# Moving the small tiles of a decoder layer so that its large SBUF tiles start at other byte offsets

## The chip, the cores and the metric

The kernel runs on one core of one Trainium2 chip. The metric is the device time of one execution in microseconds (us), the median over several runs. The kernel before takes 2655.73 us (median of three runs, 2654.69 to 2656.63).

## The reference, cut to what matters

One decoder layer on x (512 tokens of width 2048), in float32, with a memory of 256 rows:

```
q_a, k_a, v_a, q_b, k_b, v_b = split(h @ w_in)          # 2048 -> 1024+256+256+3*1024
o_a = sliding-window softmax attention with sinks (16 heads, 4 key heads)
o_b = stick-breaking attention (16 heads)
h   = layer_norm(ALPHA * h + concat(rmsnorm(o_a), rmsnorm(o_b)) @ w_o)
h   = layer_norm(ALPHA * h + cross_attention(h, mem))   # w_q_mem, w_kv_mem, w_o_mem
gate, up = split(h @ w_gate_up)                         # 2048 -> 2 * 5632
h   = layer_norm(ALPHA * h + (silu(gate) * up) @ w_down)
```

## The kernel before, in words

Nearly all of the work is matrix products on TensorE. Each float32 operand is kept as two tiles, a rounded high part and the rest (`split`, L122: ScalarE casts, VectorE subtracts), and each product is three matmuls: high with high, high with low, low with high (`mm3`, L144; `product`, L1037; `product_turned`, L1047). Every matmul loads a stationary operand of 128 by 128 (a LDWEIGHTS) and streams a moving operand of 256 or 512 columns. Each matmul has a load of its own, also where its neighbour has the same stationary operand: there are 16544 of either.

The stages follow each other in this order: the two value projections (from 0 us on), the two attentions with the query and key projections running between their pieces as filler (about 120 to 530 us), the projections of the memory (to about 730 us), the output projection (to 930 us), memory cross-attention (to about 1300 us), gate and up (L1055, to about 2190 us) and down (L1044, to the end). Gate-up and down use products of half-size blocks, seven for eight (`PRODUCTS`, L1077), with the blocks' sums made on VectorE. TensorE's and SyncE's orders are written out by hand; VectorE, ScalarE and GpSimd are ordered by the scheduler.

SBUF is laid out by pools, one after the other in the order in which they are opened (L69 to L75):

- `const`: the identity `ident`, the distances `dmt`, the block diagonal `bd`, and a few small ones.
- `px`: eight tiles of 8 KB per partition for tokens and blocks of them (x, the memory, the memory's values, h, blocks a11, a12, s4 and half of s2).
- `pm`, `pt`, `pg`: 14, 8 and 4 tiles of 4 KB (v, mix, probabilities, keys and queries, the other blocks, sums of weights).
- `pw`: nine tiles of 4 KB through which every weight passes: `ws` (as loaded), `wh` and `wl` (high and low).
- `sm`: the small tiles, that is maxima `mx`, negated maxima `nm`, sums `rs`, moments `mv`, statistics `bst`, and four `o` tiles of 2 KB.

In a product one operand of TensorE comes from `pw` (the weights) and the other from `px`, `pm`, `pt` or `pg` (the tokens). In the value, output, memory-output and down stages the tokens are stationary and the weights stream with 512 columns; in the query and key projections, the memory's projections, the key products and gate-up the weights are stationary and the tokens stream. The attention products (`avb`, `ava`, `zb`, `za`) take both operands from `pm`, `pt` and `pg`. The two matmuls of `norm` (L314, L315) are the only ones whose stationary operand, `bd`, comes from `const`.

Every slice that a matmul reads starts at a multiple of 128 floats, 512 bytes, within its tile. So where an operand starts, counted modulo 512 bytes, is a property of its pool. Before, `px`, `pm`, `pt`, `pg` and `pw` all start at 288 modulo 512, and `ident`, `dmt` and `bd` at 128.

Of the kernel before, what the change touches and what calls it, by code (L numbers as in the profile page):

```python
# [26 lines left out]
F32 = mybir.dt.float32  # L27
# [5 lines left out]
P = 128  # L33
# [24 lines left out]
def a_head(j, half):  # L58

    return 4 * (2 * (j // 4) + half) + j % 4  # L60
# [3 lines left out]
def layer(ctx, tc, io, out):  # L64
# [3 lines left out]
    PS = bass.MemoryType.PSUM  # L68
    const = ctx.enter_context(tc.tile_pool(name="const", bufs=1))  # L69
    px = ctx.enter_context(tc.tile_pool(name="px", bufs=4))  # L70
    pm = ctx.enter_context(tc.tile_pool(name="pm", bufs=14))
    pt = ctx.enter_context(tc.tile_pool(name="pt", bufs=2))
    pg = ctx.enter_context(tc.tile_pool(name="pg", bufs=4))
    pw = ctx.enter_context(tc.tile_pool(name="pw", bufs=3))
    sm = ctx.enter_context(tc.tile_pool(name="sm", bufs=2))  # L75
    banks = ctx.enter_context(ExitStack())
# [12 lines left out]
    def mtile(shape, name, dt=F32R):  # L89
        return pm.tile(shape, dt, tag="m", name=name)  # L90
# [6 lines left out]

    def otile(name, dt=F32):
        return sm.tile([P, 512], dt, tag="o", name=name, bufs=4)

    def f32(ap):
        return ap.bitcast(F32)

    def ps_z(name):
        return ps.tile([P, 2, 512], F32, tag="z", name=name, bufs=2)
# [20 lines left out]
    def urgent(f, *args, **kw):  # L126
        with tc.high_priority():
            f(*args, **kw)

    def stage(src, name):  # L130
        st = pw.tile([P, 1024], F32, tag="ws", name=f"{name}s")
        nc.sync.dma_start(st, src)
        return st
# [17 lines left out]
    def both(operands):  # L151

        heads = [operands(h, cs(h, 64)) for h in range(2)]
        for i, j in ((0, 0), (0, 1), (1, 0)):
            for acc, lhs, rhs in heads:
                nc.tensor.matmul(acc, lhs[i], rhs[j], start=(i, j) == (0, 0), stop=i == 1)

    def at(pair, *idx):
        return pair[0][idx], pair[1][idx]
# [3 lines left out]
    def cs(i, w):  # L163
        return slice(i * w, (i + 1) * w)
# [6 lines left out]
    bd = const.tile([P, P], F32R, name="bd")  # L171
    nsink = const.tile([P, 16], F32, name="nsink")
    gq = const.tile([P, 16], F32, name="gq")
    ones = const.tile([P, 1], F32, name="ones")
    nc.gpsimd.memset(ones, 1.0)

    def load_consts():
# [20 lines left out]
    for nb in range(2):  # L198
        acc = four_banks(nb, f"v{nb}")
        for u in range(8):  # L200
            if nb == 0 and u == 0:
                st, ws = pw.tile([P, 2, 512], F32, tag="ws", name="x0s"), pw.tile([P, 1024], F32, tag="ws", name="wvb0s")
# [7 lines left out]
            elif nb == 0:  # L210
                st = stage(io["xT"][u], f"x{u}").rearrange("p (c n) -> p c n", c=2)
# [177 lines left out]
    class Window:  # L389
# [6 lines left out]
        def scores(self):  # L396
            j, st = self.j, self.st
            q, k = proj["qa", j], proj["ka", j // 4]
            z = ps_z(f"za{j}_{st}")
            for b in range(2):  # L400
                n = 2 * st + b
                keys = slice(max(n - 1, 0) * P, max(n - 1, 0) * P + 256)
                both(lambda h, r: (z[:, h, cs(b, 256)], at(q, r, cs(n, P)), at(k, r, keys)))
            s = mtile([P, 2, 512], f"sa{j}_{st}", F32)
            s4 = s.rearrange("p h (b n) -> p (h b) n", b=2)
            for h in range(2):
                dist = dmt if st == 0 else dmt[:, 1:2].to_broadcast([P, 2, 256])
                slope = 2.0 ** (-8.0 * (a_head(j, h) + 1) / 16)
                nc.vector.scalar_tensor_tensor(
                    s[:, h].rearrange("p (b n) -> p b n", b=2), dist, -float(np.float32(slope)),  # L410
                    z[:, h].rearrange("p (b n) -> p b n", b=2), op0=ALU.mult, op1=ALU.add)
            mx = sm.tile([P, 4], F32, tag="mx", name=f"mx{j}_{st}")
            nm = sm.tile([P, 4], F32, tag="nm", name=f"nm{j}_{st}")
            rs = sm.tile([P, 4], F32, tag="rs", name=f"rs{j}_{st}")
            mx2 = mx.rearrange("p (h b) -> p h b", b=2)
            nm2 = nm.rearrange("p (h b) -> p h b", b=2)
            nc.vector.tensor_reduce(mx, s4, axis=AX.X, op=ALU.max)
            nsk = nsink[:, 2 * j:2 * j + 2].unsqueeze(2).to_broadcast([P, 2, 2])
            nc.vector.scalar_tensor_tensor(nm2, mx2, -1.0, nsk, op0=ALU.mult, op1=ALU.min)  # L419
            for i in range(4):  # L420
                nc.scalar.activation(s4[:, i], s4[:, i], AF.Exp, bias=nm[:, i:i + 1], accum_out=rs[:, i:i + 1])  # L421
            nc.vector.tensor_tensor(mx2, nm2, nsk, op=ALU.subtract)
            nc.scalar.activation(mx, mx, AF.Exp)
            nc.vector.tensor_tensor(rs, rs, mx, op=ALU.add)
            nc.vector.reciprocal(rs, rs)
            nc.vector.tensor_tensor(s4, s4, rs.unsqueeze(2).to_broadcast([P, 4, 256]), op=ALU.mult)
            self.s = s
# [265 lines left out]
    def ycol(t, nb):  # L693
        return y[t][nb // 2][:, cs(nb % 2, 512)]
# [4 lines left out]
    stats = {}  # L699

    def bn(name, t, nb):
        if (name, t) not in stats:
            stats[name, t] = sm.tile([P, 4, 6], F32, tag="bst", name=f"{name}st{t}", bufs=4)
        nc.vector.bn_stats(stats[name, t][:, nb], ycol(t, nb))

    for nb in range(4):
# [32 lines left out]
            y[t] = to  # L739

    def moments(t, name):
        mv = sm.tile([P, 4], F32, tag="mv", name=f"{name}mv{t}", bufs=4)
        nc.vector.bn_aggr(mv[:, 0:2], stats[name, t])
        mu, v, r0, r1 = (mv[:, i:i + 1] for i in range(4))
        nc.vector.tensor_scalar_add(v, v, LN_EPS)
        nc.scalar.activation(r0, v, AF.Ln)
        nc.scalar.activation(r0, r0, AF.Exp, scale=-0.5)
        nc.vector.scalar_tensor_tensor(r1, r0, v, r0, op0=ALU.mult, op1=ALU.mult)
        nc.vector.tensor_scalar(r1, r1, -0.5, 1.5, op0=ALU.mult, op1=ALU.add)
        nc.vector.tensor_tensor(r0, r0, r1, op=ALU.mult)  # L750
        return mu, r0

    def normalise(t, mu, r0, gb, shared, to):
        g, b = gb
        if shared:
            neg = sm.tile([P, 4], F32, tag="nm", name=f"neg{t}")[:, :1]
            nc.gpsimd.tensor_scalar_mul(neg, mu, -1.0)
        for nb in range(4):
            yc = ycol(t, nb)
            yn = to[nb // 2][:, cs(nb % 2, 512)] if to else yc  # L760
            gc, bc = g[nb // 2][:, cs(nb % 2, 512)], b[nb // 2][:, cs(nb % 2, 512)]
            if nb in shared:
                nc.scalar.activation(yn, yc, AF.Identity, bias=neg)
                nc.gpsimd.tensor_tensor(yn, yn, gc, op=ALU.mult)
                nc.scalar.mul(yn, yn, r0)
                nc.gpsimd.tensor_tensor(yn, yn, bc, op=ALU.add)
                continue
            nc.vector.scalar_tensor_tensor(yn, yc, mu, gc, op0=ALU.subtract, op1=ALU.mult)
            yield
            nc.vector.scalar_tensor_tensor(yn, yn, r0, bc, op0=ALU.mult, op1=ALU.add)  # L770
            yield
# [86 lines left out]
    def soft(hp, t, sc):  # L858

        sc = sc.rearrange("p (h m) -> p h m", h=2)  # L860
        pr = otile(f"pr{hp}_{t}").rearrange("p (h m) -> p h m", h=2)
        nm = sm.tile([P, 2], F32, tag="nm", name=f"mnm{hp}_{t}")
        rs = sm.tile([P, 2], F32, tag="rs", name=f"mrs{hp}_{t}")
        nc.vector.tensor_reduce(nm, sc, axis=AX.X, op=ALU.max)
        nc.vector.tensor_scalar_mul(nm, nm, -MEM_SCALE)
        for i in range(2):
            nc.scalar.activation(pr[:, i], sc[:, i], AF.Exp, bias=nm[:, i:i + 1], scale=MEM_SCALE,
                                 accum_out=rs[:, i:i + 1])
        nc.vector.reciprocal(rs, rs)
        nc.vector.tensor_tensor(pr, pr, rs.unsqueeze(2).to_broadcast([P, 2, M]), op=ALU.mult)  # L870

        def turn(tr):
            for i in range(2):
                for m in range(2):
                    nc.tensor.transpose(tr[:, cs(2 * i + m, P)], pr[:, i, cs(m, P)], ident)
            for i in range(2):
                h = 2 * hp + i
                if h not in pth:
                    pth[h], ptl[h] = mtile([P, 2, 512], f"pmh{h}"), mtile([P, 2, 512], f"pml{h}")
                urgent(split, pth[h][:, :, cs(t, P)], ptl[h][:, :, cs(t, P)],  # L880
                       tr[:, cs(i, 256)].rearrange("p (m n) -> p m n", m=2))
        return turn
# [115 lines left out]
    for half in range(2):  # L998
        for pair in range(2):
# [13 lines left out]
            for i in range(2):  # L1013
                for j in range(2):
                    t, nb = 2 * half + i, 2 * pair + j
# [308 lines left out]
    for i, kind in enumerate(block_kinds):  # L1324
# [15 lines left out]
        for place in order:  # L1340
            name, role = PRODUCTS[place]
# [108 lines left out]
```

## Time and profile before

| what | value |
|---|---|
| median of three runs | 2655.73 us |
| the profiled execution | 2657.68 us |
| its span, first to last instruction | 2655.9 us |
| TensorE (PE) busy | 2588.7 us, 97% |
| loads of the stationary operand (PEld) | 2329.7 us, 88%, beside PE |
| VectorE (DVE) busy | 1914.3 us, 72% |
| ScalarE (ACT) busy | 1193.5 us, 45% |
| DMA | 478.59 MB, mean 180 GB/s |

Matmuls are pipelined: the duration that a row gives for one is longer than the time until the next starts. What counts for the length of a stretch is the distance from one start to the next, called pitch below. It is read from the timeline, in which each row begins with a start in microseconds.

### The profile page before, as it was taken

The numbers are of one execution on the slowest core, as the hardware profiler recorded it, in microseconds if no ns is written. First come the engines' busy times: TensorE is split into PE (matmuls) and PEld (weight loads), VectorE is DVE, ScalarE is ACT, GpSimd is POOL, SyncE is SP. The second block draws the span as 40 slices with busy tenths as digits, with TensorE's granted clock in tenths as the row PEclk, the third lists the DMA queues.
The fourth block names the chain that finished last, engine by engine and source line by source line (L and its number), as shares of the span: only waits on it lengthen the run. The fifth ranks groups of instructions, "written<-read, shape, count | busy, mean of one in ns | idle before, by whom it ended". The sixth has DMA issues, their size and how long they took to land.

```text
span 2655.9 us, 40755 instructions
## 1 busy us (share of the span) xinstructions
PE 2588.7 (97%) x16544; PEld 2329.7 (88%) x16544; DVE 1914.3 (72%) x2170; ACT 1193.5 (45%) x1576; POOL 185.7 (7%) x324
## 2 busy tenths in 40 slices
PE   9999999999999999999999999999999998999995
PEld 7877777799988889988999999999999996877884
DVE  4258888997533574448797879887887777777788
ACT  3246656665421353334554444444445443333332
POOL 0001111010000000000000101010111001000001
PEclk9999999999999999999999999999999998999998
DMA  5322222245652483236755656563455577787763
GB/s 183 102 87 70 71 71 76 88 158 185 227 183 95 166 278 135 93 121 203 235 190 188 230 203 226 184 247 134 163 207 198 198 258 271 265 331 267 257 244 121
DMA packets 134747, 478.59 MB, mean 180 GB/s; under 512 B 16544, under 2 KB 16800, under 8 KB 133920
## 3 DMA queue, kind: packets, MB, share of 16 engines
q1 hardware_dynamic: 111024, 393.15, 42.8%
q0 software_dynamic: 23536, 82.85, 8.3%
q8 instruction: 129, 2.11, 0.3%
q14 instruction: 58, 0.48, 0.1%
HBM read 403.06 MB, written 72.88 MB: 179 GB/s over the span
## 4 chain that ended last, share of the span: by engine, by line
PE 75%; issue 12%; DVE 5%; DMA 4%; ACT 2%; POOL 1%; SPq 0%; POOLq 0%; DVEq 0%; ACTq 0%
PE zz L1055 20%; PE zz L1044 11%; PE mvp L147 1%; PE pjkb L147 1%; PE mvp L149 1%; PE mkp L149 1%; PE mkp L148 1%; PE mkp L147 1%; PE kq L149 1%; PE kq L148 1%; PE mvp L148 1%; PE kq L147 1%; PE pjqa L147 1%; PE pjkb L148 1%; PE vo L149 1%
## 5 line engine op out<-in xcount | busy, mean ns | idle before, releaser
L123 ACT CAST dn_1h<-dn_1a 128x1024 fp32r<-128x1024 f32 x44 | 46.4, 1055 | 82.5 <-PE zz L1044 73.6
L123 ACT CAST dn_0h<-dn_0a 128x1024 fp32r<-128x1024 f32 x44 | 46.0, 1052 | 77.7 <-PE zz L1044 40.6
L124 DVE TENSOR_TENSOR dn_0l<-dn_0a,dn_0h 128x1024 fp32r<-128x1024 f32 x44 | 53.4, 1220 | 21.2 <-ACT dn_0h L123 21.0
L124 DVE TENSOR_TENSOR dn_1l<-dn_1a,dn_1h 128x1024 fp32r<-128x1024 f32 x44 | 53.4, 1219 | 20.2 <-ACT dn_1h L123 20.2
L352 DVE TENSOR_TENSOR_SCAN a<-ones,nl 128x128 f32<-128x128 f32 (+3 forms) x64 | 49.8, 811 | 10.1 <-POOL nl L349 9.9
L1164 POOL DMA_DIRECT2D f_d<-fha x33 | 17.9, 542 | 407.9 <-ACT fha L123 407.5
L349 POOL TENSOR_SCALAR_AFFINE_SELECT nl<-nl 128x256 f32<-128x256 f32 x32 | 19.9, 621 | 344.3 <-DVE nl L348 344.3
L123 ACT CAST dn_0h<-dn_0b 128x1024 fp32r<-128x1024 f32 x22 | 23.2, 1054 | 45.9 <-PE zz L1044 41.5
L355 ACT ACTIVATE a<-a 128x256 f32<-128x256 f32 (+3 forms) x32 | 23.7, 739 | 38.8 <-DVE a L354 38.8
L123 ACT CAST dn_1h<-dn_1b 128x1024 fp32r<-128x1024 f32 x22 | 23.2, 1056 | 35.4 <-PE zz L1044 35.4
L421 ACT ACTIVATE sa<-sa,nm 128x256 f32<-128x256 f32 x64 | 31.9, 501 | 11.9 <-DVE nm L419 11.8
L147 PE MATMUL mvp<-mh,wmv_1h 128*128 128x256 f32 x128 | 37.1, 290 | 0.0
L600 DVE TENSOR_TENSOR dn_0a<-dn_0a,dn_0s 128x1024 f32<-128x1024 f32 x22 | 26.7, 1220 | 14.3 <-DMA dn_0s<-in_w_dn 14.2
L147 PE MATMUL mvp<-mh,wmv_0h 128*128 128x256 f32 x128 | 36.9, 288 | 0.0
L124 DVE TENSOR_TENSOR wmk_0l<-wmk_0s,wmk_0h 128x1024 fp32r<-128x1024 f32 x16 | 19.6, 1225 | 23.9 <-ACT wmk_0h L123 21.7
L149 PE MATMUL mvp<-mh,wmv_0l 128*128 128x256 f32 x128 | 36.3, 283 | 0.0
L147 PE MATMUL mkp<-mh,wmk_0h 128*128 128x256 f32 x128 | 36.2, 283 | 0.0
L148 PE MATMUL mkp<-ml,wmk_0h 128*128 128x256 f32 x128 | 36.2, 283 | 0.0
L149 PE MATMUL mkp<-mh,wmk_0l 128*128 128x256 f32 x128 | 36.2, 283 | 0.0
L147 PE MATMUL mkp<-mh,wmk_1h 128*128 128x256 f32 x128 | 36.2, 283 | 0.0
L148 PE MATMUL mkp<-ml,wmk_1h 128*128 128x256 f32 x128 | 36.2, 283 | 0.0
L149 PE MATMUL mkp<-mh,wmk_1l 128*128 128x256 f32 x128 | 36.2, 283 | 0.0
(2461 smaller groups left out, 10933.8 us busy)
## 6 DMA issues: line engine op xcount, KB each, us to landing
dn_1s<-in_w_dn SPq DMA_DIRECT2D x36, 512.0 KB, 4.7
dn_0s<-in_w_dn SPq DMA_DIRECT2D x33, 512.0 KB, 10.1
f_d<-fhs POOLq DMA_DIRECT2D x44, 256.0 KB, 2.7
f_d<-fls POOLq DMA_DIRECT2D x44, 256.0 KB, 2.9
f_d<-fha POOLq DMA_DIRECT2D x33, 256.0 KB, 5.6
f_d<-fla POOLq DMA_DIRECT2D x33, 256.0 KB, 4.8
wmv_0s<-in_w_mv SPq DMA_DIRECT2D x16, 512.0 KB, 3.4
wmv_1s<-in_w_mv SPq DMA_DIRECT2D x16, 512.0 KB, 3.3
```

What stands on the lines that cost most here:

```text
L123: nc.scalar.copy(hi, src)
L124: return nc.vector.tensor_tensor(lo, src, f32(hi), op=ALU.subtract)
L147: nc.tensor.matmul(acc, lh, rh, start=first, stop=False)
L148: nc.tensor.matmul(acc, lh, rl, start=False, stop=False)
L149: nc.tensor.matmul(acc, ll, rh, start=False, stop=last)
L349: nc.gpsimd.affine_select(out=nlt[:, :, dg], in_=nlt[:, :, dg], compare_op=ALU.is_gt, fill=0.0, base=0, channel_multiplier=1, pattern=[[0, ...
L352: nc.vector.tensor_tensor_scan(a[:, h, :nk][:, ::-1], ones.to_broadcast([P, nk]), nlt[:, h, :nk][:, ::-1], 0.0, op0=ALU.mult, op1=ALU.add)
L355: nc.scalar.activation(a[:, :, :nk], a[:, :, :nk], AF.Exp)
L421: nc.scalar.activation(s4[:, i], s4[:, i], AF.Exp, bias=nm[:, i:i + 1], accum_out=rs[:, i:i + 1])
L600: nc.vector.tensor_tensor(dst, dst, x, op=ALU.add)
L1044: nc.tensor.matmul(acc[:, t], l[:, cs(t, P)], r, start=first and c == 0 and i == 0, stop=last and c == 1 and i == 2, skip_group_check=True)
L1055: nc.tensor.matmul(z[:, j], l[:, cs(j, P)], r, start=first and c == 0 and i == 0 and j % 2 == 0, stop=last and c == 1 and i == 2, skip_gro ...
```

## The change

The program keeps every instruction, in the same order on each engine, with the same waits. What differs is addresses. Two pools are opened between the large ones: `sa`, with the tiles of `mx`, `nm` and `mv` (256 bytes in all), between `px` and `pm`, and `sb`, with those of `rs` (64 bytes), between `pg` and `pw`. `ones` (32 bytes) goes from the end of `const` to `sm`.

```
     px = ctx.enter_context(tc.tile_pool(name="px", bufs=4))
+    sa = ctx.enter_context(tc.tile_pool(name="sa", bufs=2))
     pm = ctx.enter_context(tc.tile_pool(name="pm", bufs=14))
     pt = ctx.enter_context(tc.tile_pool(name="pt", bufs=2))
     pg = ctx.enter_context(tc.tile_pool(name="pg", bufs=4))
+    sb = ctx.enter_context(tc.tile_pool(name="sb", bufs=2))
     pw = ctx.enter_context(tc.tile_pool(name="pw", bufs=3))
...
+    homes = {"mv": sa, "mx": sa, "nm": sa, "rs": sb}
+
+    def small(shape, tag, name, bufs=2):
+        return homes.get(tag, sm).tile(shape, F32, tag=tag, name=name, bufs=bufs)
...
-    ones = const.tile([P, 1], F32, name="ones")
+    ones = sm.tile([P, 1], F32, tag="ones", name="ones", bufs=1)
...
-            mx = sm.tile([P, 4], F32, tag="mx", name=f"mx{j}_{st}")
-            nm = sm.tile([P, 4], F32, tag="nm", name=f"nm{j}_{st}")
-            rs = sm.tile([P, 4], F32, tag="rs", name=f"rs{j}_{st}")
+            mx = small([P, 4], "mx", f"mx{j}_{st}")
+            nm = small([P, 4], "nm", f"nm{j}_{st}")
+            rs = small([P, 4], "rs", f"rs{j}_{st}")
```

The other places that allocated `mx`, `nm`, `rs`, `mv` or `bst` call `small` in the same way; `bst` stays in `sm`. The start of each pool's first tile, in bytes of a partition, and that modulo 512:

| pool | before | modulo 512 | after | modulo 512 |
|---|---|---|---|---|
| `const` (`ident`, `dmt`, `bd`) | 16512, 17024, 19072 | 128 | the same | 128 |
| `px` | 19744 | 288 | 19712 | 256 |
| `pm` | 85280 | 288 | 85504 | 0 |
| `pt` | 142624 | 288 | 142848 | 0 |
| `pg` | 167200 | 288 | 167424 | 0 |
| `pw` | 183584 | 288 | 183872 | 64 |
| `o` tiles of `sm` | 220448 | 288 | 220768 | 96 |

So the weights start 64 - 256 = -192, that is 320 modulo 512, behind the 8 KB tiles and 64 behind the 4 KB tiles, where both distances were 0; and all five large pools now start at multiples of 64, where they were 32 off one.

## Rows read from the trace of the kernel before

**Rows 1.** The page: span, busy time and share, granted clock in 40 slices.
```profile
span 2655.9 us, 40755 instructions
...
PE 2588.7 (97%) x16544; PEld 2329.7 (88%) x16544; DVE 1914.3 (72%) x2170; ACT 1193.5 (45%) x1576; POOL 185.7 (7%) x324
...
PEclk9999999999999999999999999999999998999998
```
**Rows 2.** The chain that ended last: shares by engine, and its longest piece (start, length).
```profile
PE 75%; issue 12%; DVE 5%; DMA 4%; ACT 2%; POOL 1%; SPq 0%; POOLq 0%; DVEq 0%; ACTq 0%
...
1755.54 414.75 PE zz L1055 x3454
```
**Rows 3.** Matmuls and loads of gate-up and down: PE and PEld busy (count), clock, DMA.
```profile
0.00:2656.00 2656.00, 891.88 (x7392) 888.17 (x7392) 0.99 0.51 180
...
0.00:2656.00 2656.00, 431.98 (x1848) 351.59 (x1848) 0.99 0.51 180
```
**Rows 4.** Timeline of gate-up, matmuls of 256 columns: start, duration, engine, line, operands.
```profile
1799.79 0.28 PE L1055 MATMUL zz<-s1l,gu6h 128*128 128x256 f32 x1
...
1800.99 0.28 PE L1055 MATMUL zz<-s1h,gu6l 128*128 128x256 f32 x1
```
**Rows 5.** Timeline of gate-up, a load beside those matmuls.
```profile
1800.03 0.19 PEld L1055 LDWEIGHTS zz<-s1l,gu6h 128*128 128x128 f32 x1
```
**Rows 6.** Timeline of the output projection, matmuls of 512 columns.
```profile
840.74 0.39 PE L147 MATMUL wo2b<-wo_3h,mixh 128*128 128x512 f32 x1
...
850.94 0.39 PE L147 MATMUL wo2a<-wo_5h,mixh 128*128 128x512 f32 x1
```
**Rows 7.** Down after a stall: timeline, and the engines' window with its granted clock.
```profile
2233.90 0.79 PE L1044 MATMUL zz<-dn_0l,s4h 128*128 128x512 f32 x1 [6.71 <-DVE dn_0l L124]
2234.49 0.63 PE L1044 MATMUL zz<-dn_0h,s4l 128*128 128x512 f32 x1
...
2236.62 0.63 PE L1044 MATMUL zz<-dn_0l,s4h 128*128 128x512 f32 x1
...
2234.40:2237.00 2.60, 2.60 (x7) 1.98 (x7) 2.60 (x3) 0.00 (x0) 0.00 (x0) 0.50 0.35 120
```
**Rows 8.** Timeline of down, after a short stall at full clock.
```profile
2523.52 0.50 PE L1044 MATMUL zz<-dn_0l,s1r 128*128 128x512 f32 x1 [0.22 <-DVE dn_0l L124]
2523.86 0.64 PE L1044 MATMUL zz<-dn_0h,s1r 128*128 128x512 f32 x2
...
2526.19 0.39 PE L1044 MATMUL zz<-dn_0h,s2h 128*128 128x512 f32 x1
...
2526.87 0.39 PE L1044 MATMUL zz<-dn_0h,s2h 128*128 128x512 f32 x1
```
**Rows 9.** Timeline of gate-up, after a short stall at full clock.
```profile
1368.50 0.28 PE L1055 MATMUL zz<-s1h,gu3h 128*128 128x256 f32 x1
...
1369.33 0.28 PE L1055 MATMUL zz<-s1l,gu3h 128*128 128x256 f32 x1
...
1369.93 0.28 PE L1055 MATMUL zz<-s1h,gu3h 128*128 128x256 f32 x1
```
**Rows 10.** Timeline of the attention stage around the two matmuls with `bd`.
```profile
370.19 0.39 PE L149 MATMUL pjqa<-xh,wqa_0l 128*128 128x512 f32 x1
...
371.10 0.39 PE L314 MATMUL ms<-sq,bd 128*128 128x512 f32 x1
371.33 0.39 PE L315 MATMUL ms<-sq,bd 128*128 128x512 f32 x1
...
372.72 0.39 PE L149 MATMUL pjqa<-xh,wqa_1l 128*128 128x512 f32 x1
```
**Rows 11.** Groups of VectorE: operands, shapes, count, busy us, mean ns, idle before.
```profile
L409 DVE SCALAR_TENSOR_TENSOR sa<-dmt,za 128x512 f32<-128x512 f32 x32 | 21.0, 675 | 2.5 <-PE za L156 2.5
...
L124 DVE TENSOR_TENSOR kb<-pjkb,kb 128x512 fp32r<-128x512 f32 x8 | 5.5, 682 | 0.0
```

More of the change, by code (lines that the diff above doesn't have):

```diff
@@ L702, in bn @@
         if (name, t) not in stats:
-            stats[name, t] = sm.tile([P, 4, 6], F32, tag="bst", name=f"{name}st{t}", bufs=4)
+            stats[name, t] = small([P, 4, 6], "bst", f"{name}st{t}", bufs=4)
         nc.vector.bn_stats(stats[name, t][:, nb], ycol(t, nb))
@@ L741, in moments @@
     def moments(t, name):
-        mv = sm.tile([P, 4], F32, tag="mv", name=f"{name}mv{t}", bufs=4)
+        mv = small([P, 4], "mv", f"{name}mv{t}", bufs=4)
         nc.vector.bn_aggr(mv[:, 0:2], stats[name, t])
@@ L755, in normalise @@
         if shared:
-            neg = sm.tile([P, 4], F32, tag="nm", name=f"neg{t}")[:, :1]
+            neg = small([P, 4], "nm", f"neg{t}")[:, :1]
             nc.gpsimd.tensor_scalar_mul(neg, mu, -1.0)
@@ L861, in soft @@
         pr = otile(f"pr{hp}_{t}").rearrange("p (h m) -> p h m", h=2)
-        nm = sm.tile([P, 2], F32, tag="nm", name=f"mnm{hp}_{t}")
-        rs = sm.tile([P, 2], F32, tag="rs", name=f"mrs{hp}_{t}")
+        nm = small([P, 2], "nm", f"mnm{hp}_{t}")
+        rs = small([P, 2], "rs", f"mrs{hp}_{t}")
         nc.vector.tensor_reduce(nm, sc, axis=AX.X, op=ALU.max)
```

## The prediction, made before the changed kernel ran

> **What bounds the kernel now.** I read the page first. TensorE is busy for 97% of the span at the full clock almost throughout [rows 1], and 75% of the chain that ended last is its work, with one unbroken piece of 414.75 us in gate-up [rows 2]. So the time is the number of matmuls by their pitch, plus some stalls. The change leaves the number alone; only the pitch, or the speed of another engine or of a transfer, can move.
>
> Next the timeline, for the pitch. In gate-up, ten matmuls of 256 columns start within 1.20 us [rows 4]: 120.0 ns each, and the long piece says the same, 414.75 us / 3454 = 120.1 ns [rows 2]. In the output projection 45 matmuls of 512 columns start within 10.20 us [rows 6]: 226.7 ns. After a long stall the granted clock is 0.50, the lower level of 1.2 GHz, and five matmuls of 512 columns start within 2.13 us [rows 7]: 426 ns, which is 512 columns / 1.2 GHz = 426.7 ns with nothing on top. At the upper level, 2.4 GHz, streaming alone would be 213.3 ns for 512 columns and 106.7 ns for 256. So each matmul at the full clock takes 13.3 ns more than its columns, whichever its size. A load of the next stationary operand starts with every matmul [rows 4, 5], so two streams are read from SBUF at once, and the 13.3 ns may be what they cost each other. That is the only thing in this profile on which a change of addresses could act at a price worth having.
>
> How much there is: gate-up has 7392 matmuls of 256 columns and down 1848 of 512 [rows 3]. By the loops, lines 147 to 149 have 968 each of 256 columns (64 values, 136 attention, 512 memory projections, 256 key products) and 1184 each of 512 (128 values, 416 query and key projections, 256 output, 128 each for the memory's values times its output weights, scores and attention output); `norm` has 32. That makes 10296 of 256 columns and 5432 of 512, and 15728 x 13.3 ns = 209 us of excess in a span of 2655.9 us.
>
> **Is the excess a matter of addresses?** For: it isn't a fixed price. After a short stall the ten matmuls of 512 columns from 2523.86 us on take 233 ns each (2.33 us), and then three take 0.68 us, 227 ns again [rows 8]. In gate-up seven after a stall take 0.83 us, 118.6 ns, and then five take 0.60 us, 120 ns [rows 9]. So the pitch depends on how the two streams fall against each other, and it settles. The only loads from another offset modulo 512 are those of `bd`. Ahead of them four matmuls took 0.91 us, 227.5 ns; from the first of them on, seven took 1.62 us, 231.4 ns [rows 10]: they upset the settled state. Against: the settled pitch returns every time, to the same value, and it holds through changes of weight tile, bank and product in rows 6; whatever the upset, no stretch stays under 226.7 ns for 512 columns or under about 118 ns for 256. A system that finds its way back to one pitch from any start in time is likely to do so from another start in address.
>
> The Trainium skill speaks against the change here: "SBUF — State Buffer", section "Who interferes with whom", gives TensorE two independent read ports, one for the moving operand and one for the load, so that neither waits. By that the excess isn't contention, any address is as good as any other, and the sum is 0; rows 8 and 10 agree with it only in part, since there the pitch does move.
>
> **The change part by part.**
> - Instructions, order, waits: the same, so 0 by themselves.
> - TensorE: 15728 matmuls at a new distance between their operands' starts: 320 or 64 modulo 512 where weights are stationary, 192 or 448 where they stream, 0 still in the attention products, 128 at `bd`. The trace has no operand at these distances, so I bound it. Best end: the excess goes, 13.3 ns x (10296 + 4184) = 193 us, where 4184 leaves out the 3 x 416 projections amid attention, which are rarely settled. Worst end: all stay as upset as after `bd`, +4.7 ns on the same 14480 matmuls, 68 us. Near the middle: every stream upset as in rows 8 and 9 gives 4184 x (233 - 226.7) = +26 us and 10296 x (118.6 - 120) = -14 us, together +12 us. I take 0: the settled pitch comes back.
> - VectorE, ScalarE, GpSimd: their operands move with the pools. VectorE's instruction on `dmt`, which starts at 128 modulo 512, with a result at 288, takes 675 ns; one of the same size with all SBUF operands at 288 takes 682 ns [rows 11]. The addresses aren't felt, within 1%. VectorE has 5% of the chain [rows 2], 133 us; 1% of that is 1.3 us either way. I take 0, hidden by TensorE; if that cover went (a pitch under 110 ns), VectorE's 1914 us would still fit beside it.
> - Transfers: a row of 4 KB that starts 32 bytes off a multiple of 64 touches 65 pieces of 64 bytes, afterwards 64. DMA has 4% of the chain [rows 2], 106 us; 1/65 of that is 1.6 us to gain at most. No row shows it as a difference, and I take 0.
> - The small tiles that move are of 16 and 8 bytes in instructions whose count doesn't change: 0.
>
> Sum: 0. The profiled execution took 2657.68 us, the span 2655.9 us of it; the median of the runs, 2655.73 us, is 1.95 us under the profiled execution. The forecast is for the median: 2655.7 us.
>
> **The rivals.**
> 1. Slower: the streams never settle. Between products of gate-up and down the distance switches between the 8 KB and the 4 KB tiles (320 and 64, or 192 and 448), and within s2, whose high part lies in `pm` and whose low part in `px`, it switches from matmul to matmul. For it: the two `bd` matmuls alone cost five more at an upset pitch. Against: in gate-up a settled and an upset pitch are nearly equal. It decides once 512 columns stay at 231.4 ns: 4184 x 4.7 ns = 20 us, so about 2676 us; 2724 us if 256 columns lose as much. Chance 0.24.
> 2. Faster in part: the distance keeps the streams out of each other's way some of the time. Rows 9 are an upset that pays, 118.6 ns: 10296 x 1.4 ns = 14 us, about 2641 us. Half the excess gone is 97 us, about 2559 us. For it: the excess moves, and equal starts on both sides are one special case. Against: nothing in the trace holds such a pitch. Chance 0.24.
> 3. Faster outright: more than half of the excess goes, at best all, 193 us, about 2463 us, and stalls that are now covered would show. For it: at the lower clock there is no excess, so the streaming itself needs none. The Trainium skill would have it so: "TensorE: Matmul & The Clock Gate", section "Back-to-back issue gap", gives columns / 2.4 + 2.5 ns, that is about 216 ns for 512; the trace's 226.7 ns doesn't agree. Against: the settled state never comes near it. Chance 0.12.
> 4. That the change doesn't do what it says: the addresses are settled before the run and the instructions are equal. No chance is left for it.
>
> **How the numbers follow.** No difference has the remaining chance, 0.40, with 2651 to 2661 us as its own range (0.2%, 5.3 us, is about what a measurement of this kernel can tell from no change). Faster is 0.24 + 0.12 = 0.36, slower 0.24. The prediction is that of the likeliest case, 2655.7 us. The range reaches down to half of the excess gone, 2558 us, leaving out rival 3 (0.12), and up to 2690 us, past rival 1's 2676 us by a third of the way to 2724 us; I leave 0.05 above it.
>
> **What would show each step right or wrong.** If I am right, gate-up's timeline shows 120 ns and the output projection's 226.7 ns again, stage by stage, and the span is unchanged. If rival 1 holds, rows of 512 columns read 230 ns and more in the output projection and in down, and s2's stretches are the worst. If rivals 2 or 3 hold, gate-up's pitch is under 118 ns and its long piece shorter by that share. A pitch that differs between products from `px` and from `pm` tiles of one stage would show that the distance decides, and my step that the settled pitch comes back would be the one that failed. A change in VectorE's 682 ns or in landings with an unchanged pitch would mean that I looked at the wrong reader.

## The result and the profile after

The changed kernel takes 2635.84 us (median of 6 runs, 2624.23 to 2641.77) against 2655.44 us before (6 runs, 2652.19 to 2656.63). The ratio is 0.9918, 95% interval 0.9903 to 0.9933: some 20 us, 0.8%, faster. That is inside the range, but not the likeliest case: I had given "no difference" 0.40 and this case, faster in part, 0.24. The profiled execution took 2641.77 us, 15.9 us less than before's 2657.68 us, so the difference of the two traces is a little smaller than that of the medians; it is the longest of the six runs, so what its trace shows need not be what the median run did.

The page of the changed kernel, the same lines as [rows 1] and [rows 2] show, one of its groups and one of its issues:

```profile
span 2640.1 us, 40755 instructions
...
PE 2565.3 (97%) x16544; PEld 2293.0 (87%) x16544; DVE 1913.7 (72%) x2170; ACT 1192.7 (45%) x1576; POOL 185.7 (7%) x324
...
PEclk9999999999999999999999999999999999999998
...
PE 68%; issue 16%; DVE 6%; DMA 5%; ACT 3%; POOL 2%; SPq 0%; POOLq 0%; DVEq 0%; ACTq 0%
...
L131 DVE TENSOR_TENSOR dn_1l<-dn_1a,dn_1h 128x1024 fp32r<-128x1024 f32 x44 | 53.5, 1220 | 22.1 <-ACT dn_1h L130 22.1
...
dn_0s<-in_w_dn SPq DMA_DIRECT2D x33, 512.0 KB, 9.9
```

The number of instructions is the same, and VectorE and ScalarE are busy for as long as before (1913.7 against 1914.3 us, 1192.7 against 1193.5 us). The split of a weight tile on VectorE takes 1220 ns (1219 before) and the landing of `dn_0s` 9.9 us (10.1 before). TensorE alone has changed, and its share of the chain fell from 75% to 68%. The lines stand 7 further down in the changed kernel: gate-up is L1062, down L1051, `mm3` L154 to L156, `split` L130 and L131. The same windows as in [rows 3], gate-up and then down:

```profile
0.00:2641.00 2641.00, 864.87 (x7392) 859.32 (x7392) 0.99 0.51 181
...
0.00:2641.00 2641.00, 437.81 (x1848) 353.40 (x1848) 0.99 0.51 181
```

Gate-up's matmuls are busy for 27.0 us less (891.88 before), down's for 5.8 us more (431.98 before). The timeline of TensorE shows why: the output projection, two stretches of gate-up with the row of a wait between them, and two stretches of down. Columns as in [rows 4]; what stands in brackets is the idle time before the row and what ended it.

```profile
797.75 0.39 PE L155 MATMUL wo1b<-wo_3l,mixh 128*128 128x512 f32 x1
...
808.97 0.39 PE L156 MATMUL wo1b<-wo_5h,mixl 128*128 128x512 f32 x1
...
1699.43 0.28 PE L1062 MATMUL zz<-a22l,gu5h 128*128 128x256 f32 x1
...
1705.10 0.28 PE L1062 MATMUL zz<-a22h,gu5h 128*128 128x256 f32 x1
...
1791.30 0.28 PE L1062 MATMUL zz<-s2l,gu6h 128*128 128x256 f32 x1
...
1792.32 0.28 PE L1062 MATMUL zz<-s2l,gu6h 128*128 128x256 f32 x1
1793.20 0.39 PE L1062 MATMUL zz<-s2h,gu6l 128*128 128x256 f32 x1 [0.60 <-DVE gu6l L131]
1793.42 0.28 PE L1062 MATMUL zz<-s2h,gu6h 128*128 128x256 f32 x1
1793.54 0.28 PE L1062 MATMUL zz<-s2l,gu6h 128*128 128x256 f32 x1
...
1794.72 0.28 PE L1062 MATMUL zz<-s2h,gu6l 128*128 128x256 f32 x1
...
1899.42 0.28 PE L1062 MATMUL zz<-s3h,gu7h 128*128 128x256 f32 x1
...
1905.19 0.28 PE L1062 MATMUL zz<-a12l,gu7h 128*128 128x256 f32 x1
...
2299.63 0.39 PE L1051 MATMUL zz<-dn_1h,s3l 128*128 128x512 f32 x1
...
2310.84 0.39 PE L1051 MATMUL zz<-dn_1h,a12h 128*128 128x512 f32 x1
...
2449.28 0.40 PE L1051 MATMUL zz<-dn_1h,s4l 128*128 128x512 f32 x1
...
2460.48 0.40 PE L1051 MATMUL zz<-dn_1h,s3l 128*128 128x512 f32 x1
```

- Output projection: 49 matmuls in 11.22 us, 229.0 ns each, where [rows 6] have 226.7.
- Gate-up at 1700 us: 50 in 5.67 us, 113.4 ns, where [rows 4] have 120.0. At 1900 us: 49 in 5.77 us, 117.8 ns. These are two settled pitches of the same work. The switch is at 1793.20 us: up to the wait nine matmuls take 1.02 us (113.3 ns), and from 1793.54 us on, ten take 1.18 us (118 ns), within one product, s2 with gu6. After that, over 3100 matmuls in a row stay at 117.8 ns, to the end of gate-up. I count a matmul as settled where nine distances in a row have one of the two pitches as their mean, within 0.7 ns: of gate-up's 7392 matmuls 3275 have 113.3 ns and 4018 have 117.8. The pitch changes from one to the other eleven times, each time at a stall.
- Down: 49 in 11.21 us, 228.8 ns, from s3 into a12; and 48 in 11.20 us, 233.3 ns, from s4 into s3. Here too a tile from `pm` and one from `px` have the same pitch, and there are two settled pitches: by the same count 970 matmuls of down have 228.9 ns and 794 have 233.3.

Laid against each other matmul by matmul, from start to start, the two traces differ by -15.8 us. Outside stalls (a distance under 130 ns for 256 columns and under 250 ns for 512 in both traces) there are 10,179 matmuls of 256 columns, 119.91 to 115.88 ns in the mean, -41.0 us, and 5169 of 512 columns, 227.84 to 230.44 ns, +13.4 us. The other 1195 distances, stalls above all, make +11.8 us. Of these last, gate-up has the most: what its matmuls take beyond their mean pitch where they wait went from 11.1 to 23.0 us. So gate-up gained 7392 x 4.17 ns = 30.8 us by its pitch and is 18.9 us shorter. The waits of TensorE between 1320 and 2200 us (what was waited for: us in total, times, longest) before:

```profile
PE zz L1055 <- DVE gu1l L124: 1.2, 3, 0.6
PE zz L1055 <- DVE gu0l L124: 1.1, 3, 0.6
...
PE zz L1055 <- DVE gu2l L124: 0.7, 2, 0.6
PE zz L1055 <- DVE gu3l L124: 0.4, 1, 0.4
```

and after:

```profile
PE zz L1062 <- DVE gu1l L131: 3.0, 4, 0.9
PE zz L1062 <- DVE gu2l L131: 3.0, 4, 1.3
PE zz L1062 <- DVE gu0l L131: 2.8, 4, 1.3
...
PE zz L1062 <- DVE gu3l L131: 0.6, 1, 0.6
PE zz L1062 <- DVE gu6l L131: 0.6, 1, 0.6
PE zz L1062 <- DVE gu4l L131: 0.4, 1, 0.4
```

TensorE waits for the low half of a weight tile, the last step of its split, for 10.4 us where it was 3.4. The split itself takes as long as before; TensorE arrives earlier. This view counts idle time alone: it names 7.0 of the 11.9 us that gate-up lost at stalls, and the rest isn't broken down here.

### The profile page after: what moved, and what is told of

It is laid out like the page before. It is cut to its first block, busy times and chain, and to the rows that moved or that the text cites. A ratio compares the mean times of both kernels' runs of the same rounds, so it can differ in the third digit from the quotient of the medians.

```text
span 2640.1 us, 40755 instructions
## 1 busy us (share of the span) xinstructions
PE 2565.3 (97%) x16544; PEld 2293.0 (87%) x16544; DVE 1913.7 (72%) x2170; ACT 1192.7 (45%) x1576; POOL 185.7 (7%) x324
## 4 chain that ended last, share of the span: by engine, by line
PE 68%; issue 16%; DVE 6%; DMA 5%; ACT 3%; POOL 2%; SPq 0%; POOLq 0%; DVEq 0%; ACTq 0%
PE zz L1062 14%; PE zz L1051 12%; DMA dn_0s<-in_w_dn 1%; PE pjkb L154 1%; PE pjqa L154 1%; PE kq L156 1%; PE kq L154 1%; PE pjkb L155 1%; PE kq L155 1%; PE vo L154 1%; PE vo L155 1%; PE vo L156 1%; POOL f_d L1171 1%; PE pjkb L156 1%; PE pjqa L155 1%
## 5 line engine op out<-in xcount | busy, mean ns | idle before, releaser
L130 ACT CAST dn_1h<-dn_1a 128x1024 fp32r<-128x1024 f32 x44 | 46.2, 1050 | 82.8 <-PE zz L1051 70.3
L130 ACT CAST dn_0h<-dn_0a 128x1024 fp32r<-128x1024 f32 x44 | 45.9, 1049 | 76.9 <-PE zz L1051 44.1
L131 DVE TENSOR_TENSOR dn_1l<-dn_1a,dn_1h 128x1024 fp32r<-128x1024 f32 x44 | 53.5, 1220 | 22.1 <-ACT dn_1h L130 22.1
L131 DVE TENSOR_TENSOR dn_0l<-dn_0a,dn_0h 128x1024 fp32r<-128x1024 f32 x44 | 53.4, 1221 | 21.9 <-ACT dn_0h L130 21.8
L359 DVE TENSOR_TENSOR_SCAN a<-ones,nl 128x128 f32<-128x128 f32 (+3 forms) x64 | 49.8, 811 | 10.1 <-POOL nl L356 9.9
L130 ACT CAST dn_0h<-dn_0b 128x1024 fp32r<-128x1024 f32 x22 | 23.1, 1049 | 46.0 <-PE zz L1051 43.4
L130 ACT CAST fhs<-f 128x512 fp32r<-128x512 f32 x44 | 27.3, 620 | 31.3 <-DVE f L980 23.8
L130 ACT CAST dn_1h<-dn_1b 128x1024 fp32r<-128x1024 f32 x22 | 23.1, 1051 | 36.6 <-PE zz L1051 33.1
L131 DVE TENSOR_TENSOR wmk_0l<-wmk_0s,wmk_0h 128x1024 fp32r<-128x1024 f32 x16 | 19.6, 1226 | 26.8 <-ACT wmk_0h L130 26.7
L154 PE MATMUL mkp<-mh,wmk_0h 128*128 128x256 f32 x128 | 35.9, 280 | 1.7 <-DVE ktl L131 1.7
L154 PE MATMUL mvp<-mh,wmv_1h 128*128 128x256 f32 x128 | 36.7, 287 | 0.0
L154 PE MATMUL mvp<-mh,wmv_0h 128*128 128x256 f32 x128 | 36.4, 285 | 0.0
L355 DVE SCALAR_TENSOR_TENSOR nl<-zb,nl 128x256 f32<-128x256 f32 (+3 forms) x32 | 26.3, 822 | 13.3 <-ACT nl L354 13.2
L156 PE MATMUL mvp<-mh,wmv_0l 128*128 128x256 f32 x128 | 35.8, 280 | 0.0
L155 PE MATMUL mvp<-ml,wmv_1h 128*128 128x256 f32 x128 | 35.7, 279 | 0.0
L156 PE MATMUL mvp<-mh,wmv_1l 128*128 128x256 f32 x128 | 35.7, 279 | 0.0
L155 PE MATMUL mvp<-ml,wmv_0h 128*128 128x256 f32 x128 | 35.7, 279 | 0.0
```

Of the source, the lines that this page charges most:

```text
L130: nc.scalar.copy(hi, src)
L131: return nc.vector.tensor_tensor(lo, src, f32(hi), op=ALU.subtract)
L154: nc.tensor.matmul(acc, lh, rh, start=first, stop=False)
L155: nc.tensor.matmul(acc, lh, rl, start=False, stop=False)
L156: nc.tensor.matmul(acc, ll, rh, start=False, stop=last)
L355: nc.vector.scalar_tensor_tensor(nl, zz, 0.0, nl, op0=ALU.max, op1=ALU.add)
```

## The experiments

The theory after the result: the settled pitch depends on the distance in bytes between the start of the stationary operand and that of the moving one. Rivals: the multiples of 64 count (alignment), or what ran before counts.

**The distance by itself.** The layer is left out. Chains of 40 matmuls, with tokens' start and distance set by slices, once behind two and once behind three other matmuls:

```
+    def run(n, base, delta, count, acc):
+        for i in range(count):
+            m0 = base // 4 + 512 * (i % 2)
+            s0 = (base + delta) % 512 // 4 + 128 * (i % 4)
+            nc.tensor.matmul(acc[:, :n], sta[:, s0:s0 + P], mov[:, m0:m0 + n], start=i == 0, stop=i == count - 1)
```

> This kernel leaves the whole layer out: it copies one piece of x to the output and runs chains of 40 matmuls, each chain with one distance (start of the stationary operand less start of the moving one, modulo 512 bytes) and one width (256 or 512 columns), at 30 pairs of start and distance, twice over, after 2 or after 3 matmuls of the other width. Theory D (the distance sets the settled pitch): at distance 0 256 columns settle at 120 ns and 512 at 226.7 ns; at 64 and 320 256 columns settle at 113 or 118 ns; at 192 and 448 512 columns settle at 229 to 233 ns, at 256 at 227 ns; starting the moving operand 32 bytes further, with the same distance, changes nothing. Rival A (alignment to 64 bytes is what counts): with the moving operand at 0 all distances that are multiples of 64 give one pitch per width, 113 to 118 ns and 229 to 233 ns, and with the moving operand at 32 they give 120 and 226.7 ns. Rival H (only the history counts): the pitches differ between the two passes and not between distances.

Measured in one run of 904.87 us, in ns from start to start, mean of each chain's last part; where the two passes differ both stand:

```
distance      0      32     64     96           128          160    192    224
256 columns   120.0  118.3  113.3  117.5/117.3  118.8/120.0  120.0  117.8  117.8/116.7
512 columns   226.7  233.3  233.3  234.2        232.1        233.3  228.9  233.3
```

Distances 256 to 480 gave the same row again, with a difference of 0.1 at most: the period is 256 bytes. With the tokens' start at 32 in place of 0 the pitches are the same, but for 117.8 instead of 113.3 ns in one of two passes at 64, and 118.5 to 118.7 (256 columns) and 233.3 in one pass (512 columns) at 128. Six chains per width at distances off this grid (4, 16, 48, 80, 240 and 272) show that what ran before has a part too: most gave the same pitch in both passes, but with 256 columns distance 48 gave 123.3 ns in one and 117.8 in the other, and distance 240 gave 120.0 and 117.3. So in this sweep the distance sets the pitch, in places together with what ran before, and alignment does nothing that shows. The timeline groups the matmuls of a chain; two groups, distances 0 and 64, each with the chain of 40 and two of the matmuls ahead of it:

```profile
451.21 5.41 PE L95 MATMUL acc<-mov,sta 128*128 128x512 f32 x42
...
462.13 5.17 PE L95 MATMUL acc<-mov,sta 128*128 128x512 f32 x42
```

The second is 0.24 us shorter, 6 ns for each of the 40. Most of the layer's numbers fit the table. Modulo 256, the change puts the stages of 256 columns at 64 (113.3 or 117.8 ns) and most of those of 512 at 192 (228.9). The 233.3 ns in parts of down don't: no chain at 192 shows them. The trace also holds a control: in the scores of memory cross-attention (`kq` with h, no weight tile) the change moves the distance from 0 to 256, which is 0 modulo 256, and these matmuls of 512 columns keep their mean of 227.8 ns (227.7 after). The 8 KB tiles at 320 and the 4 KB tiles at 64 are the same case, which is why nothing happens where the two meet.

**Alignment alone in the layer.** Only `ones` moves, so all large pools start at 256 modulo 512, a multiple of 64, with distance 0:

```
-    ones = const.tile([P, 1], F32, name="ones")
+    ones = sm.tile([P, 1], F32, tag="ones", name="ones", bufs=1)
```

> The kernel before with one edit: ones goes from the end of const to sm, so all five large pools start at 256 modulo 512, multiples of 64, with distance 0 between weights and tokens as before. Theory D (distance): no change, 2655 us within 0.2%, gate-up at 120.0 ns and the output projection at 226.7 ns. Rival A (alignment): the whole gain of the change, about 2636 us, gate-up at 113 to 118 ns.

2654.38 us, ratio 0.9993 (0.9984 to 1.0003). The timeline of its gate-up, twelve matmuls in 1.44 us, 120.0 ns:

```profile
1799.52 0.28 PE L1055 MATMUL zz<-s1l,gu6h 128*128 128x256 f32 x1
...
1800.96 0.28 PE L1055 MATMUL zz<-s1l,gu6h 128*128 128x256 f32 x1
```

**The distances without the alignment.** The change, but `ones` stays in `const`, so every large pool lies 32 off a multiple of 64:

```
-    ones = sm.tile([P, 1], F32, tag="ones", name="ones", bufs=1)
+    ones = const.tile([P, 1], F32, name="ones")
```

> The changed kernel with ones put back at the end of const, so px starts at 288, pm, pt and pg at 32 and pw at 96 modulo 512: the distances 320 and 64 stay, but every large pool is 32 bytes off a multiple of 64. Theory D (distance): as the change, 2624 to 2642 us, gate-up at 113 and 118 ns. Rival A (alignment): back to 2655 us, gate-up at 120.0 ns.

2633.47 us, 0.9908 (0.9892 to 0.9925): the whole gain is there. The distance carries it; no share of alignment shows.

**Each small pool alone.** With `sb` alone all tokens lie 64 from the weights; with `sa` alone the distances are 256 and 0. In the change:

```
-    homes = {"mv": sa, "mx": sa, "nm": sa, "rs": sb}
+    homes = {"rs": sb}
```

and

```
-    homes = {"mv": sa, "mx": sa, "nm": sa, "rs": sb}
+    homes = {"mv": sa, "mx": sa, "nm": sa}
```

> Half of the change: sb stays (64 bytes before the weights), sa is left empty, so the weights lie 64 behind all token tiles, px, pm, pt and pg alike. By the sweep's map, which repeats every 256 bytes, 64 and 320 are one and the same: as the change, 2624 to 2642 us. Rival (the two kinds of token tiles have to differ, 320 and 64): a clearly smaller gain, 2645 us or more.

> The other half: sa stays (256 bytes between px and pm), sb is left empty, so the weights lie 256 behind the 8 KB tiles and 0 behind the 4 KB tiles. By the sweep's map 256 is as 0: 120.0 ns and 226.7 ns, 2655 us within 0.2%. Rival (period 512, any shift of the 8 KB tiles counts): half of the gain, about 2645 us.

`sb` alone: 2641.45 us (2632.15 to 2649.61), 0.9934 (0.9915 to 0.9953), an interval that overlaps the change's. `sa` alone: 2655.72 us, 0.9996 (0.9987 to 1.0005), and gate-up's mean pitch is 119.98 ns, as before. The 64 bytes of `rs` carry the gain; 256 bytes are no distance, in the layer as in the sweep.

**Another distance.** `mx`, `nm` and `rs` all in `sb`: 192 where weights are stationary, 64 where they stream, so the two columns of the table change places:

```
-    homes = {"mv": sa, "mx": sa, "nm": sa, "rs": sb}
+    homes = {"mx": sb, "nm": sb, "rs": sb}
```

> mx, nm and rs (192 bytes) lie ahead of the weights and sa is empty, so the weights lie 192 behind all token tiles. By the sweep's map 256 columns with stationary weights stand at 117.8 ns in place of 120 (10296 x 2.2 = 23 us less), and 512 columns with streaming weights at distance 64, 233.3 ns in place of 226.7 (about 3900 x 6.6 = 26 us more); the projections among the attention are taken as unchanged: about 2659 us, from 2650 to 2668. Rival (any distance that isn't 0 helps the whole): 2645 us or less.

2655.74 us, 0.9999 (0.9990 to 1.0008). Its timeline, gate-up and down:

```profile
1798.74 0.28 PE L1062 MATMUL zz<-s1l,gu6h 128*128 128x256 f32 x1
...
1804.98 0.28 PE L1062 MATMUL zz<-s2h,gu6h 128*128 128x256 f32 x1
...
2449.28 0.39 PE L1051 MATMUL zz<-dn_1l,s1h 128*128 128x512 f32 x1
...
2460.48 0.39 PE L1051 MATMUL zz<-dn_1l,s2h 128*128 128x512 f32 x1
```

53 in 6.24 us, 117.7 ns, and 48 in 11.20 us, 233.3 ns: the pitches of the table. Over the trace, outside stalls, 10,190 matmuls of 256 columns gained 2.3 ns and 5178 of 512 lost 4.5 ns, 23 us each way, which cancel. This time without a difference says nothing against the theory: both terms are in the trace.

**Steps of 4 bytes, and what sets which of the two pitches.** The layer is left out again; chains of 30 at each distance from 0 to 252, then chains of 36 at distance 64 behind different matmuls ("kicks"), four times each:

```
+    for n in (256, 512):
+        for delta in range(0, 256, 4):
+            run(768 - n, 0, 0, 2, accs[1])
+            run(n, 0, delta, 30, accs[0])
...
+            run(256, 0, 64, 36, accs[0])
```

> This kernel leaves the whole layer out and copies a piece of x to the output. First it runs a chain of 30 matmuls for each distance from 0 to 252 bytes in steps of 4, with 256 and with 512 columns; then chains of 36 matmuls of 256 columns at distance 64, each behind a short disturbance (one matmul of another width, 1 to 5 of 512 columns, 1 to 4 of 128, one at another distance), each disturbance four times over. Theory D: the low pitches are narrow, 120 and 226.7 ns within a few bytes of 0, 113.3 ns within a few bytes of 64. Theory B (two settled states at distance 64): the chains end at 113.3 or at 117.8 ns and at nothing between, and which one depends on the disturbance and on the state before it. Rival: the two pitches drift from one to the other within a chain, so that chains average between them.

In one run of 1238.84 us: 113.3 ns for 256 columns came at 64, 76 and 88 alone; at 60 and 68 it was 119.9 and 118.4. 512 columns had 226.7 ns at 0, 36, 100, 120, 132, 156, 204, 240, 244 and 252, and 228.9 to 238.0 elsewhere. So the pitch changes from 4 bytes to the next, and the low pitch of 512 columns is not confined to the neighbourhood of 0, as I had expected. Each distance had one chain here, though, and 512 columns at 240 had 228.3 ns in both passes of the sweep: single entries of this map can depend on what ran before. The chains of 36 at distance 64 ended at 113.3 or 117.8 ns, never between. One kick of 256 columns at distances 96 to 224 led to 113.3 each time, at 0, 32 or 64 to 117.8 each time; 248 columns and four kicks of 512 always to 117.8; one, two, three or five of 512 always to 113.3; and one of 64, 96, 160, 192, 240, 264 or 320 columns now to one, now to the other.

**Kicks in the layer.** An extra matmul into a spare bank ahead of the second step of a product: with `bd` (distance 128) in three products of seven, 30 in all; in all seven, 71; and as a control 30 with a slice of the weights (distance 64). Then the change once more on the same chip. The extra matmuls' result is not used.

```
+            if kick and c == 1:
+                nc.tensor.matmul(junk[:, :256], bd, ah, start=True, stop=True)
```

> The changed kernel with 30 more matmuls: in the products a11, s2 and s3 of every gate-up block (s2 and s3 of the partial ones), between the first unit's two halves, one matmul of 256 columns with bd as stationary operand (distance 128 to the token tiles) into a PSUM tile that nobody reads. Theory B (two settled states, and a matmul at distance 96 to 224 leads to the lower one, as in the chains of e4): gate-up stands at 113.3 ns behind each of them until the next stall. In the profiled run of the change 4006 of gate-up's matmuls stood at 117.8 ns, 18 us above 113.3; the extra matmuls cost 30 x 0.12 = 4 us; so 2618 to 2630 us, and closer together from run to run. Rival (the state is set by something else in the layer): the time of the change plus 4 us, 2628 to 2646 us.

> As e8, with such a matmul in every product of gate-up, 71 in all. Theory B: stalls are followed sooner by the lower state, for 71 x 0.12 = 8.5 us: 2618 to 2632 us, not clearly apart from e8. Rival (state set by something else): 2632 to 2650 us.

> The control of e8: the same 30 matmuls at the same places, with the unit's own weights (its first 128 columns) as stationary operand, so at distance 64 as all others. Theory B with D (only another distance upsets the state; in e4 one matmul at distance 64 kept 117.8 ns): no help, the time of the change plus 4 us, 2628 to 2646 us, gate-up partly at 117.8 ns. Rival (any extra matmul upsets the state): as e8.

> The changed kernel itself on the chip of e8 to e10, for its spread: 2624 to 2642 us, each run with its own mix of 113.3 and 117.8 ns in gate-up.

```
                 median us  range               ratio   95%               gate-up at 113.3 / 117.8
30 with bd       2638.30    2633.44 to 2647.37  0.9933  0.9916 to 0.9950  6090 / 1108
71 with bd       2645.23    2638.98 to 2651.16  0.9952  0.9935 to 0.9970  2958 / 4241
30, distance 64  2643.11    2640.35 to 2649.81  0.9948  0.9932 to 0.9964  4831 / 2429
the change       2640.81    2630.44 to 2647.25  0.9929  0.9912 to 0.9946   722 / 6594
```

Two misses; the intervals of the first row and of the change nearly coincide. In the profiled executions 30 kicks have most of gate-up at 113.3 ns, but 71 have less than half of it there, and the control, which kept 117.8 ns in the chains, has two thirds. The same changed kernel had 3275 matmuls at 113.3 ns in its first trace and 722 in this one, so one trace of each kernel can't tell what a kick does in the layer; that it decides isn't borne out. And a shorter pitch is not all gain: the profiled executions of the first row and of the change differ by 23.8 us of pitch in gate-up but took 2638.16 and 2647.25 us, 9.1 us apart, and the medians are 2.5 us apart. The waits of TensorE between 1320 and 2200 us with 30 kicks of `bd`:

```profile
PE zz L1064 <- DVE gu0l L131: 3.6, 5, 1.0
PE zz L1064 <- DVE gu1l L131: 3.2, 4, 1.6
PE zz L1064 <- DVE gu2l L131: 2.6, 4, 1.4
...
PE zz L1064 <- DVE gu10l L131: 1.6, 2, 1.3
...
PE zz L1064 <- DVE gu3l L131: 0.9, 1, 0.9
PE zz L1064 <- DVE gu4l L131: 0.7, 1, 0.7
```

12.6 us of waits for splits, at a mean pitch of 114.1 ns. Over all kernels with the layer, gate-up's mean pitch, what stalls add, and the sum of its 7392 distances, each from the profiled execution:

```
                     pitch ns  stalls us  sum us
256 and 0 (sa)       119.98    12.7       899.6
alignment alone      119.98    11.6       898.5
before               119.98    11.1       898.0
distance 192         117.78    16.5       887.1
the change, again    117.35    18.7       886.1
64 for all (sb)      117.18    21.3       887.6
distance 12 (below)  116.69    18.3       880.9
the change, 32 off   116.44    22.2       882.9
71 kicks with bd     116.06    26.0       883.9
the change           115.81    23.0       879.1
30 kicks, control    114.87    27.8       876.9
30 kicks with bd     114.13    27.8       871.4
```

From `before` to the last row 43.2 us of pitch became 26.6 us of time; the rest went into stalls.

**A distance that is cheap for both sizes.** Of the steps of 4 bytes, 12 has 116.7 ns for 256 columns and its opposite, 244, has 226.7 for 512. The pools' starts above are all multiples of 32, so `wh` and `wl` became slices of one tile, in the kernel before:

```
+    places = ph.tile([P, 6 * 1024 + 8], F32R, tag="hl", name="hl")
...
+        return [places[:, 3 + 1024 * i:1027 + 1024 * i] for i in (k, k + 3)]
...
-        hi = pw.tile([P, 1024], F32R, tag="wh", name=f"{name}h")
-        lo = pw.tile([P, 1024], F32R, tag="wl", name=f"{name}l")
+        hi, lo = whl()
```

> The kernel before with the six weight tiles wh and wl as slices of one larger tile that begin 12 bytes into it, so that every weight operand starts 12 bytes behind the tokens (modulo 256); instructions and their order stay. Where weights stream, the distance is 244. The steps of 4 bytes showed 116.7 ns for 256 columns at 12, 226.7 ns for 512 columns at 244 and 230.0 ns for 512 columns at 12 (the query and key projections). Theory (the distance alone sets the pitch, and a chain of 30 matmuls shows the one that the layer gets): 9696 x 3.3 ns = 32 us less for 256 columns, nothing for the 3768 of 512 columns at 244, up to 1248 x 3.3 ns = 4 us more for the projections, some 8 us of new waits in gate-up as in the change; about 2636 us, 2626 to 2646, with down's start-to-start at 226.7 ns, where the change has 230.9. Rival 1 (the chains of 30 don't carry over: the layer's stalls put the streams into other states at this distance): gate-up between 117 and 120 ns, down over 228 ns, 2645 to 2660 us. Rival 2 (a start that is no multiple of 32 bytes costs VectorE, ScalarE or the transfers): VectorE's split of 128x1024, 1220 ns before, over 1235 ns, and waits for gu..l and dn..l that eat the gain: 2655 us or more.

2637.90 us (2634.89 to 2642.03), 0.9931 (0.9917 to 0.9944), as the theory had it (2636). The timeline, gate-up and down (`hl` is the tile of the slices; a row with x2 and one with x1 make three matmuls):

```profile
1801.79 0.28 PE L1062 MATMUL zz<-s2l,hl 128*128 128x256 f32 x1
...
1804.94 0.27 PE L1062 MATMUL zz<-s2l,hl 128*128 128x256 f32 x1
...
2453.27 0.62 PE L1051 MATMUL zz<-hl,s4h 128*128 128x512 f32 x2
...
2460.14 0.62 PE L1051 MATMUL zz<-hl,s3h 128*128 128x512 f32 x2
```

Gate-up: 27 in 3.15 us, 116.7 ns, as in the chains of 30. Down: 30 in 6.87 us, 229.0 ns, where the chains had 226.7; there rival 1 was right, and the layer settles otherwise. So the forecast of the time hit with one term off: against before, the trace has -31.1 us for 256 columns (expected -32), +7.6 for 512 (expected 0 to 4) and +8.0 for the rest (expected 8). None of the versions is faster than the change beyond its interval.

## Where the prediction was wrong and where right, step by step

The measured time lies inside the range, but that is its width: from 2558 to 2690 us it held the likeliest case and both signs of a partial effect. The likeliest case itself, no difference, didn't come, and its mechanism was wrong.

- **The step that failed** is "I take 0: the settled pitch comes back". A settled pitch does come back after each disturbance, as [rows 6, 8, 9] had shown, but its value goes with the distance: 120.0 ns at 0 and 113.3 or 117.8 at 64 (256 columns), 226.7 at 0 and 228.9 at 192 (512 columns). I had concluded from a return after disturbances in time that a change of address would be undone too. The trace before held only one distance in its settled stretches, 0 modulo 256, so it couldn't tell. The term that I put at 0 measured -41.0 us for 256 columns and +13.4 for 512, with +11.8 us of new stalls behind it.
- **The rule against the change.** The Trainium skill, "SBUF — State Buffer", section "Who interferes with whom", gives TensorE's two reads independent ports. The sweep doesn't agree with what I drew from it, that any address is as good as another: with the same columns the pitch goes from 113.3 to 120.0 ns by distance. The formula that rival 3 took from the Trainium skill ("TensorE: Matmul & The Clock Gate", section "Back-to-back issue gap") is given there for an isolated matmul, not for a stream of loads and matmuls as here; no settled stretch of any run is under 226.7 ns for 512 columns.
- **The sizes.** Both signs of my "near the middle" sum were right, and neither size: +26 us for 512 columns measured +13.4, -14 us for 256 columns measured -41.0. My prices came from upset stretches, 233 and 118.6 ns; the settled ones are 228.9 (233.3 in part) and 113.3 to 117.8. The counts were a little high: 10296 and 4184 hold 408 attention products and 384 scores of the memory, whose distance stayed 0 modulo 256. The sum had no term for new stalls, +11.8 us: I had named them for rival 3 alone, though nothing in their cause needs so large a gain.
- **Rival 2** is what came, by its mechanism, and its 2641 us is near the measured 2635.84. That nearness is luck: its single term of 14 us stands where -41.0, +13.4 and +11.8 us nearly make the same sum. What I held against it, "nothing in the trace holds such a pitch", was true of the trace before alone. **Rival 1** came as well, as the smaller term: the mean of down rose from 226.9 to 230.9 ns in the first trace of the change, to 229.1 in the second. But its mechanism, streams that never settle since the distance switches between tiles, isn't there: 320 and 64 are one case, and the pitch holds from `pm` to `px`.
- **The right terms.** Instructions, VectorE, ScalarE and transfers: 0, and their rows didn't move. Of the 32 bytes and the 65th piece nothing shows either: alignment alone gave 0.9993 (0.9984 to 1.0003).
- **The sign to look for** was badly chosen. I expected a difference between products from `px` and from `pm` if the distance counted; with a period of 256 there is none.
- The projections amid attention, left out as rarely settled, took part: 231.0 to 233.2 ns in the mean, +2.3 us of the +13.4.

**What stays open.** Which of the two pitches a stretch takes after a stall in the layer: in the chains some kinds of kick decide it reproducibly, in the layer that isn't shown. The spread of the change's runs, 2624 to 2642 us where before has 2652 to 2657, would fit it, since 7392 x 4.5 ns = 33 us lie between the two pitches, and the two profiled executions of the change do differ (115.81 and 117.35 ns in gate-up), but the other runs show no pitches. Nor is it known where down's 233.3 ns come from. Why the pitch goes with the distance isn't shown; that the two reads hold each other up is a guess. A distance of 64 for the stages of 256 columns with 0 for those of 512 wasn't tried: the weights' pool would have to move between gate-up and down. By down's 1848 x 4.0 ns (230.9 less 226.9) it would be worth some 7 us there, an estimate from the first trace; from the second, 229.1 ns, it is 4 us.

## What to carry to other kernels

Where TensorE loads a new stationary operand with every float32 matmul, as here (no other type was tried), look at the distance between the two operands' starts modulo 256 bytes, read the pitch from start to start at two or three distances, and do it for each number of columns, since a distance that helps one size can cost the other. A pitch that is the same everywhere in a trace is no floor if every place in that trace has the same addresses. And a shorter pitch is worth what the engines that feed TensorE can keep up with: here 30.8 us of pitch in gate-up gave 18.9 us of time.

## What the runs showed of the hardware that I had not expected

- The pitch of float32 matmuls with a load each depends on the distance of the operands' starts, with a period of 256 bytes: 113.3 to 120.0 ns for 256 columns, 226.7 to 234.2 ns for 512 in steps of 32. It changes from one step of 4 bytes to the next (119.9, 113.3, 118.4 ns at 60, 64, 68, one chain each).
- The two sizes don't go together: of the steps of 32, distance 64 is the best for 256 columns and among the worst for 512 (233.3 ns); distance 0 is the best for 512 and among the worst for 256.
- At one distance there can be two settled pitches, 113.3 and 117.8 ns, kept over more than 3100 matmuls; all eleven changes between them in the first trace of the change stand at a stall.
- A start 12 bytes into a tile costs VectorE and ScalarE, which write the weights there, nothing that shows: they were busy for 1914.7 and 1191.3 us, before for 1914.3 and 1193.5. No transfer touches these slices, so the run says nothing on transfers.
